# A decoder block on one Trainium2 core: its first projection taken by feature tiles instead of by output units

## The chip, the cores and the metric

The kernel runs on one core of one Trainium2 chip. The core has a matrix engine (TensorE, PE in the profile, with its weight loads as PEld), a vector engine (VectorE, DVE), an activation engine (ScalarE, ACT), a general engine (GpSimd, POOL) and a queue engine that issues the transfers (SyncE, SP), each with its own instruction stream, and sixteen DMA engines. The metric is the time of one execution in microseconds of the device, the median of several runs. Less is better.

## The reference, cut to what matters

Input is one sequence of 1024 positions with 1024 features and a conditioning vector `c`. Everything is float32.

```python
c_act = silu(c)
cond = c_act @ ada_w + ada_b                       # 1024 x 6144
shift1, scale1, gate1, shift2, scale2, gate2 = split(cond, 6)

h = rmsnorm(x, norm1_g) * (1 + scale1) + shift1
z = h @ w_in + b_in                                # 1024 x 2048
u, v, val, gate = split(z, [512, 1024, 1536])
y_a = spatial_gating_mixer(gelu(u), gelu(v), ...)  # layer norm of v, 128 x 128 mixing per head
y_b = conformer_conv_mixer(val, gate, ...)         # val*sigmoid(gate), 31-tap conv, group norm, silu
y = concat(rmsnorm(y_a), rmsnorm(y_b))
x = x + gate1 * (y @ w_out)

h2 = rmsnorm(x, norm2_g) * (1 + scale2) + shift2
g, up = split(h2 @ w_ffn_in, 2)                    # 1024 x 5632
x = x + gate2 * ((silu(g) * up) @ w_ffn_out)
return rmsnorm(x, norm_f_g) * (1 + scale_f) + shift_f
```

## The kernel before

Features lie on the 128 partitions, so `x` is eight tiles `x0` to `x7` of 128 features by 1024 positions. The positions are worked on in two halves of 512. A float32 product is made of three matmuls on values rounded to the fast matmul format: each operand is split into a rounded part (`hi`, a copy made by ACT) and the remainder (`lo`, a subtraction), and `mm3` (lines 588 to 592) adds `hi·hi`, `lo·hi` and `hi·lo` into one PSUM bank. `weights` (line 566) loads 128x1024 numbers of a weight, lets ACT make `wh` and an engine of the caller's choice make `wl` (line 574).

The first phase makes `val` and `gate` of the first half. It needs `h1_0_k`, the normed and modulated input of feature tile k, and for that the two condition columns of the tile: shift and scale. A column is a product of 128x1024 numbers of `ada_w` with `cact` summed along the row (`ada_cols`, line 546, a DVE instruction with an accumulator); the numbers are loaded into the four `ypad` tiles, which later hold the input of the convolution. `finish_shift` and `finish_scale` (lines 557, 561, 562) add the bias and the norm's gain, three DVE instructions of one column. `modulated` (lines 602, 612, 613) makes the tile: DVE multiplies `x` with scale and the inverse root `r1a`, ACT adds the shift and rounds, DVE makes the remainder.

Eight PSUM banks hold the eight results `p{j}_{vg}` (four column groups j of `val` and of `gate`) through the whole phase. The weights come in eight units of 128 columns over all 1024 input features (`wvg`), one for each bank, so a feature tile k can be used for the banks whose unit has arrived: tile 0 for j = 0, tile 1 for j = 0 and 1 and tile 0 for the new j = 1, and so on; from tile 3 on each tile goes into all eight banks. POOL makes the `wl` of these units. The loop over the last tile takes j in the order 3, 2, 0, 1, and `glu` (lines 660, 662) then empties the banks into `ypad` in that order.

After it follow, for the rest of the mixer: `u` of the first half (banks `pu`), the second norm (`rstd`, lines 628 to 647: ACT squares, a matmul with ones sums over the features, ACT and DVE make the inverse root `rt_n`, a matmul of line 641 spreads it over 128 rows), the second half's `h1`, `v`, the spatial mixing, the convolution (`cv`, lines 851 and 854, on DVE, six of its 31 taps by ACT and POOL in lines 845 and 846), its group norm (`gn`, line 871), the output projection. `v` has the positions on the partitions, so its bias cannot come with the activation; it is added by one more matmul to each of the eight groups (line 753), whose operands `vsel` and `vb` have 33 rows: row 0 carries the bias, row 32 its remainder. The feed-forward network (lines 904 to 1180) is a scheme of seven products `A`, `B`, `C` in place of eight; a part of its first matmuls (`ah`) is done ahead, in the middle of the mixer.

The order of the instructions on each engine is not the order of the code. `fix_order` (line 440) takes all instructions, simulates them with a table of costs (`duration`, line 122, and the class `Clock`, line 304) and keeps a list schedule: at each step the engine that is free first takes the ready instruction with the longest path behind it. Transfers take part as instructions of SP. `Slots` says which buffer a tile gets; memory that pools share in time is handed over by `hand_over`. The order so found is then fixed on each engine.

## Time and profile before

| | |
|---|---|
| median of 3 runs | 1009.9 us (1009.88 to 1010.12) |
| the profiled execution: its time | 1013.1 us |
| its span, first to last instruction | 1011.4 us |
| PE busy | 967.0 us, 96% |
| PEld busy | 776.3 us, 77% |
| DVE busy | 876.9 us, 87% |
| ACT busy | 466.0 us, 46% |
| POOL busy | 421.4 us, 42% |
| mean granted clock of PE | 0.990 |
| share of the chain that ended last: PE, DVE, DMA, ACT, issue | 82%, 7%, 5%, 3%, 2% |

The span is what the trace shows; the time of that execution is 1.7 us more, and 3.2 us above the median of the runs without a profile. An engine's busy share is a mean over the whole span, and the stages differ: the first phase lies between 24.44 us, where the first matmul of a bank `p` starts, and 80.96 us, where the first `pu` starts. The mean clock of 0.990 is made of long stretches at full speed and short ones near half of it, so it has to be read for a stretch and not for the run. In the rows below, the idle time in square brackets is that of the engine before the instruction, with what ended it.

### The profile page before, as it was taken

The page shows a single profiled execution, that of the slowest core. Times are in us where ns is not written, and L with a number is a line of the kernel's source. Part 1 is how long each engine was busy: PE and PEld are TensorE (multiplying, and loading weights), DVE is VectorE, ACT ScalarE, POOL GpSimd, SP SyncE. Part 2 cuts the span into 40 slices and gives each one's busy share as a digit, 9 for nine tenths or more (in the row PEclk, how much of TensorE's full clock was granted, in tenths as well). Part 3 has the DMA queues.
Part 4 walks back from the last instruction along what each step waited for, and adds up shares of the span by engine and source line. Part 5 has one row for each costly group of instructions (what it writes and reads, how often), then busy time and mean ns, then how long its engine had stood idle before and what let it go on. Part 6 is the DMA issues. An engine that isn't in the chain of part 4 may idle for free.

```text
span 1011.4 us, 13149 instructions
## 1 busy us (share of the span) xinstructions
PE 967.0 (96%) x4613; PEld 776.3 (77%) x4613; DVE 876.9 (87%) x1216; ACT 466.0 (46%) x727; POOL 421.4 (42%) x240
## 2 busy tenths in 40 slices
PE   3799899999999999999999999999999999999994
PEld 1587677778878877788887888888888788888873
DVE  5978999899999736499999999999978989969946
ACT  5237747653375364365432333333336437226426
POOL 2618698773727410385344555444543100000121
PEclk9899999999999999999999999999999999999997
DMA  9854063343556633583577767776748918415104
GB/s 340 324 191 146 21 212 101 106 132 106 158 195 199 198 115 108 185 309 107 177 229 250 248 223 247 243 249 216 253 173 289 357 49 268 142 32 176 33 0 167
DMA packets 73567, 183.89 MB, mean 182 GB/s; under 512 B 8188, under 2 KB 10492, under 8 KB 73502
## 3 DMA queue, kind: packets, MB, share of 16 engines
q1 hardware_dynamic: 73502, 183.06, 53.6%
q8 instruction: 36, 0.59, 0.2%
q14 instruction: 29, 0.24, 0.1%
HBM read 141.87 MB, written 41.16 MB: 181 GB/s over the span
## 4 chain that ended last, share of the span: by engine, by line
PE 82%; DVE 7%; DMA 5%; ACT 3%; issue 2%; POOL 1%; SPq 0%; ACTq 0%; DVEq 0%; POOLq 0%
PE B L913 28%; PE C L913 16%; PE ah L913 10%; PE A L913 3%; PE po L591 3%; PE po L590 3%; PE po L592 3%; PE p L590 2%; PE p L591 2%; PE p L592 2%; PE v L590 2%; PE v L591 1%; PE v L592 1%; DMA ypad<-ada 1%; DVE fa L906 1%
## 5 line engine op out<-in xcount | busy, mean ns | idle before, releaser
L913 PE MATMUL B<-h,w_f 128*128 128x512 f32 x816 | 189.5, 389 | 0.7 <-DVE x L1132 0.7
L913 PEld LDWEIGHTS B<-h,w_f 128*128 128x128 f32 x816 | 153.0, 188 | 32.9 <-DVE x L1132 1.1
L851 DVE SCALAR_TENSOR_TENSOR cv<-ypad,colt,cv 128x512 f32<-128x512 f32 x216 | 147.1, 746 | 0.1
L913 PE MATMUL B<-fa,w_d 128*128 128x512 f32 x528 | 126.5, 390 | 1.4 <-DVE fa L906 1.0
L913 PE MATMUL C<-h,w_f 128*128 128x512 f32 x528 | 123.7, 389 | 0.0
L913 PEld LDWEIGHTS B<-fa,w_d 128*128 128x128 f32 x528 | 98.7, 188 | 23.8 <-DVE fa L906 1.9
L913 PEld LDWEIGHTS C<-h,w_f 128*128 128x128 f32 x528 | 99.1, 188 | 20.6
L913 PE MATMUL ah<-h,wh_a 128*128 128x512 f32 x320 | 100.9, 393 | 0.2 <-ACT sg L660 0.2
L1194 POOL TENSOR_TENSOR sq_nf<-sq_nf,sq_nf 128x512 f32<-128x512 f32 x9 | 12.6, 1395 | 184.7 <-ACT sq_nf L1189 184.7
L905 ACT ACTIVATE w_f<-raw_f 128x512 fp32r<-128x512 f32 x68 | 42.4, 630 | 97.3 <-PE B L913 52.0
L905 ACT ACTIVATE w_d<-raw_d 128x512 fp32r<-128x512 f32 (+1 forms) x72 | 42.1, 593 | 86.5 <-PE B L913 37.3
L574 POOL TENSOR_TENSOR wl_a<-raw_a,wh_a 128x1024 fp32r<-128x1024 f32 x20 | 49.2, 2462 | 70.8 <-ACT wh_a L573 69.8
L1155 POOL TENSOR_TENSOR x<-x,up 128x512 f32<-128x512 f32 x20 | 34.9, 1744 | 96.0 <-ACT x L1154 96.0
L913 PEld LDWEIGHTS ah<-h,wh_a 128*128 128x128 f32 x320 | 59.9, 188 | 14.7 <-issue 1.5
L906 DVE TENSOR_TENSOR w_f<-raw_f,w_f 128x512 fp32r<-128x512 f32 x68 | 67.0, 990 | 1.4 <-ACT w_f L905 1.4
L913 PE MATMUL C<-fa,w_d 128*128 128x512 f32 (+1 forms) x273 | 64.6, 384 | 0.0
L913 PE MATMUL ah<-h,wl_a 128*128 128x512 f32 x160 | 62.7, 394 | 0.0
L590 PE MATMUL p<-h,wh_vg 128*128 128x512 f32 x128 | 53.4, 423 | 9.3 <-ACT h L612 8.6
L913 PEld LDWEIGHTS C<-fa,w_d 128*128 128x128 f32 x273 | 50.0, 188 | 10.8 <-issue 1.0
L574 POOL TENSOR_TENSOR wl_vg<-raw_vg,wh_vg 128x1024 fp32r<-128x1024 f32 x16 | 43.4, 2728 | 35.3 <-ACT wh_vg L573 35.3
L906 DVE TENSOR_TENSOR fa<-a,fa 128x512 fp32r<-128x512 f32 x77 | 54.0, 741 | 0.2 <-ACT fa L905 0.2
L1262 DVE SCALAR_TENSOR_TENSOR x<-B,cond,x 128x512 f32<-128x512 f32 x48 | 35.8, 747 | 20.2 <-PE B L913 20.0
(223 smaller groups left out, 2142.3 us busy)
## 6 DMA issues: line engine op xcount, KB each, us to landing
acts<-x SPq DMA_DIRECT2D x77, 256.0 KB, 3.0
a<-acts SPq DMA_DIRECT2D x77, 256.0 KB, 4.3
raw_f<-wf SPq DMA_DIRECT2D x32, 512.0 KB, 3.9
ada<-ada SPq DMA_DIRECT2D x24, 512.0 KB, 3.7
x<-ada SPq DMA_DIRECT2D x24, 512.0 KB, 3.5
...
```

Of the source, the lines that this page charges most:

```text
L574: lo_eng.tensor_tensor(lo, raw, hi.bitcast(F32), op=ALU.subtract)
L590: PE.matmul(acc, shi, mhi, start=start, stop=False)
L591: PE.matmul(acc, slo, mhi, start=False, stop=False)
L592: PE.matmul(acc, shi, mlo, start=False, stop=stop)
L851: V.scalar_tensor_tensor(accs[j], src, wc, accs[j], op0=ALU.mult, op1=ALU.add)
L905: A.activation(dst[:, 0, :], src, AF.Copy)
L906: lo_eng.tensor_tensor(dst[:, 1, :], src, dst[:, 0, :].bitcast(F32), op=ALU.subtract)
L913: last_mm = PE.matmul(bank[:, cols], s, m[:, cols], start=first and p == 0 and i == 0, stop=p == n - 1 and i == 2, skip_group_check=True)
L1155: G.tensor_tensor(g0, g0, up0, op=ALU.mult)
L1194: G.tensor_tensor(sums[half], sums[half], t, op=ALU.add)
L1262: V.scalar_tensor_tensor(xs[k][:, part], bank[:, cols], ccol(GATE2, k), xs[k][:, part], op0=ALU.mult, op1=ALU.add)
```

## The change

The first phase goes by feature tiles. A new input `wk` holds rows 128k to 128k+127 of `w_in[:, 1024:]`, so one load of 128x1024 numbers serves tile k for all eight banks. For each k the kernel makes the two condition columns, splits `wk[k]` (the remainder on DVE instead of POOL), makes the tile and takes its 24 matmuls, j = 0 to 3; `glu` empties the banks in that order. The three small DVE instructions of a tile become two ACT instructions of one column (`Identity` with scale and bias), with `gain` made once on DVE. The tile itself is made by DVE (x times r), ACT (times scale plus shift), ACT (rounding copy) and DVE (remainder). The first norm's squares are no longer added in pairs on DVE: each goes to a matmul of its own, and the warming square root stands behind the second Silu. The bias of `v` has 128 rows, of which rows 0 and 32 count as before.

In the scheduler, a transfer holds SP until its queue would run dry in `DMA_AHEAD` = 0.5 us, so that what is issued next is chosen later; a matmul that uses part of the array costs 0.09 or 0.12 us more where it follows one of the other kind; three PE durations differ; and memory that pools share is handed over at one moment, when all tiles of the earlier pools are free.

```diff
@@ Step, duration, Clock
+        self.partial = self.engine == "PE" and (self.reads[0].box[1] - self.reads[0].box[0] < P
+                                                or self.reads[1].width < P)
-            t = {128: 0.213, 32: 0.16}.get(m, 0.115)
+            t = {128: 0.219, 32: 0.068}.get(m, 0.109)
-            t = n / 600
+            t = 0.857
-            self.free["SP"] = t + DMA_ISSUE
+            self.free["SP"] = max(t + DMA_ISSUE, self.queue - LOAD_WAIT - DMA_AHEAD)
+        if s.engine == "PE" and s.partial != self.partial:
+            self.partial = s.partial
+            t += 0.09 if s.partial else 0.12
@@ Slots.hand_over
+        if self.in_use or not self.waits_for:
+            return []
@@ block_kernel
-        A.activation(cact[:, hs(h)], cb, AF.Silu)
+        silu = A.activation(cact[:, hs(h)], cb, AF.Silu).ins
     warm = const.tile([P, 1], F32, name="warm")
-    A.activation(warm, epst, AF.Sqrt)
+    with issue_after(silu):
+        A.activation(warm, epst, AF.Sqrt)
-    vb = front.tile([33, DA], F32R, name="vb")
-    vsel = front.tile([33, 1], F32R, name="vsel")
+    vb = front.tile([P, DA], F32R, name="vb")
+    vsel = front.tile([P, 1], F32R, name="vsel")
-        raw = tmp("vb_raw")[0:33]
-        nc.sync.dma_start(raw, vbias.partition_broadcast(33))
+        raw = tmp("vb_raw")
+        nc.sync.dma_start(raw, vbias.partition_broadcast(P))
-    r1a = rstd(x_half(0), D, "n1_0", (2, 2, 2, 2), V, True)
+    r1a = rstd(x_half(0), D, "n1_0", (1,) * 8, None, True)
+    gain = const.tile([P, KD], F32, name="gain")
+    V.scalar_tensor_tensor(gain, bcol(SCALE1, 0, KD), 1.0, colt[:, _OFF["norm1_g"]:_OFF["norm1_g"] + KD],
+                           op0=ALU.add, op1=ALU.mult)
     for k in range(KD):
-        ada_cols(SHIFT1 * 8 + k, dst=ypad[2 * k % 4][:, HALO:HALO + D])
-        ada_cols(SCALE1 * 8 + k, dst=ypad[(2 * k + 1) % 4][:, HALO:HALO + D])
-        if k < 4:
-            for vg in range(2):
-                w8[k, vg] = weights(wvg[2 * k + vg], f"vg{vg}_{k}", G, "act" if k >= 2 else "w")
-        finish_shift(SHIFT1, k, 1)
-        finish_scale(SCALE1, "norm1_g", k, 1)
-        h1[0][k] = modulated(0, k, r1a, SHIFT1, SCALE1, f"h1_0_{k}")
-        for j in range(min(k + 1, 4)) if k < KD - 1 else (3, 2, 0, 1):
-            for kk in range(k + 1) if (j == k) else (k,):
-                for vg in range(2):
-                    mm3(acc[j, vg], unit(w8[j, vg], kk), full(h1[0][kk]), kk == 0, kk == KD - 1)
-    for j in (3, 2, 0, 1):
+        for m, g in ((SCALE1, 0), (SHIFT1, 1)):
+            ada_cols(m * 8 + k, dst=ypad[(2 * k + g) % 4][:, HALO:HALO + D])
+        w_k = weights(wk[k], f"k{k}", V)
+        A.activation(ccol(SCALE1, k), ccol(SCALE1, k), AF.Identity, bias=gain[:, k:k + 1], scale=col("norm1_g", k))
+        A.activation(ccol(SHIFT1, k), ccol(SHIFT1, k), AF.Identity, bias=bcol(SHIFT1, k))
+        t = tmp(f"t_h1_0_{k}")
+        V.tensor_tensor(t, xs[k][:, hs(0)], r1a, op=ALU.mult)
+        A.activation(t, t, AF.Identity, bias=ccol(SHIFT1, k), scale=ccol(SCALE1, k))
+        h = h1[0][k] = act_tile(f"h1_0_{k}", 0)
+        A.activation(h[:, 0, :], t, AF.Copy)
+        V.tensor_tensor(h[:, 1, :], t, h[:, 0, :].bitcast(F32), op=ALU.subtract)
+        for j in range(4):
+            for vg in range(2):
+                mm3(acc[j, vg], unit(w_k, 4 * vg + j), full(h), k == 0, k == KD - 1)
+    for j in range(4):
         glu(j, 0, acc[j, 0], acc[j, 1])
-            PE.matmul(bank, vsel.broadcast_to([33, P]), vb, start=False, stop=True)
+            PE.matmul(bank, vsel.broadcast_to([P, P]), vb, start=False, stop=True)
```

On SP, the transfers that follow the first half of `x` stood in this order before (`ypad` gets columns of `ada_w`, `raw_vg` the units of the weight, `x0` to `x7` here are the second half of `x`, which only the second norm needs):

```order
L541 DMA ypad1_107<-ada 128x1024
L541 DMA ypad0_106<-ada 128x1024
L509 DMA colt_74<-cols 128x277
L541 DMA ypad3_109<-ada 128x1024
L541 DMA ypad2_108<-ada 128x1024
L568 DMA raw_vg0_0_177<-wvg 128x1024
L568 DMA raw_vg1_0_183<-wvg 128x1024
L568 DMA raw_vg0_1_207<-wvg 128x1024
L937 DMA x0_76<-xT 128x512
L937 DMA x1_77<-xT 128x512
L937 DMA x2_78<-xT 128x512
L937 DMA x3_79<-xT 128x512
```

and now (`raw_k` is the row block of tile k):

```order
L521 DMA colt_74<-cols 128x277
L554 DMA ypad0_106<-ada 128x1024
L554 DMA ypad1_107<-ada 128x1024
L581 DMA raw_k0_191<-wk 128x1024
L554 DMA ypad2_108<-ada 128x1024
L554 DMA ypad3_109<-ada 128x1024
L581 DMA raw_k1_233<-wk 128x1024
L554 DMA ypad0_106<-ada 128x1024
L554 DMA ypad1_107<-ada 128x1024
L581 DMA raw_k2_275<-wk 128x1024
L554 DMA ypad2_108<-ada 128x1024
L554 DMA ypad3_109<-ada 128x1024
```

The second half of `x` has moved behind the first phase's loads; each tile's two columns and its weight now stand side by side.

On DVE, in the middle of the first phase, the work for tiles 3 to 5 was this before (`ypad` rows are condition columns, `t_h1` and `h1` the tile and its remainder, the 128x1 rows bias and gain):

```order
L602 SCALAR_TENSOR_TENSOR t_h1_0_3_318<-x3_79,cond_105,r_n1_0_163 128x512
L613 SCALAR_TENSOR_TENSOR h1_0_3_320<-t_h1_0_3_318,cond_105,h1_0_3_320 128x512
L546 SCALAR_TENSOR_TENSOR ypad1_107,cond_105<-ypad1_107,cact_96 128x1024
L546 SCALAR_TENSOR_TENSOR ypad0_106,cond_105<-ypad0_106,cact_96 128x1024
L561 TENSOR_TENSOR cond_105<-cond_105,colt_74 128x1
L546 SCALAR_TENSOR_TENSOR ypad3_109,cond_105<-ypad3_109,cact_96 128x1024
L562 SCALAR_TENSOR_TENSOR cond_105<-cond_105,colt_74 128x1
L557 TENSOR_TENSOR cond_105<-cond_105,colt_74 128x1
L561 TENSOR_TENSOR cond_105<-cond_105,colt_74 128x1
L602 SCALAR_TENSOR_TENSOR t_h1_0_4_372<-x4_80,cond_105,r_n1_0_163 128x512
L546 SCALAR_TENSOR_TENSOR ypad2_108,cond_105<-ypad2_108,cact_96 128x1024
L613 SCALAR_TENSOR_TENSOR h1_0_4_374<-t_h1_0_4_372,cond_105,h1_0_4_374 128x512
```

and now:

```order
L725 TENSOR_TENSOR t_h1_0_3_325<-x3_79,r_n1_0_175 128x512
L587 TENSOR_TENSOR wl_k3_320<-raw_k3_317,wh_k3_319 128x1024
L559 SCALAR_TENSOR_TENSOR ypad0_106,cond_105<-ypad0_106,cact_96 128x1024
L729 TENSOR_TENSOR h1_0_3_328<-t_h1_0_3_325,h1_0_3_328 128x512
L559 SCALAR_TENSOR_TENSOR ypad1_107,cond_105<-ypad1_107,cact_96 128x1024
L725 TENSOR_TENSOR t_h1_0_4_367<-x4_80,r_n1_0_175 128x512
L587 TENSOR_TENSOR wl_k4_362<-raw_k4_359,wh_k4_361 128x1024
L559 SCALAR_TENSOR_TENSOR ypad2_108,cond_105<-ypad2_108,cact_96 128x1024
L729 TENSOR_TENSOR h1_0_4_370<-t_h1_0_4_367,h1_0_4_370 128x512
L559 SCALAR_TENSOR_TENSOR ypad3_109,cond_105<-ypad3_109,cact_96 128x1024
```

The small rows have gone to ACT, and each tile now has the weight's remainder `wl_k` on DVE: five rows for one tile.

On DVE around the second norm, whose inverse root is `rt_n1_1` and whose tiles are `t_h1_1`, the order before was (`cv` the convolution, `ada22` a later condition column):

```order
L851 SCALAR_TENSOR_TENSOR cv0_1_1130<-ypad1_107,colt_74,cv0_1_1130 128x512
L851 SCALAR_TENSOR_TENSOR cv0_0_1129<-ypad0_106,colt_74,cv0_0_1129 128x512
L546 SCALAR_TENSOR_TENSOR ada22_969,cond_105<-ada22_969,cact_96 128x1024
L851 SCALAR_TENSOR_TENSOR cv0_1_1130<-ypad1_107,colt_74,cv0_1_1130 128x512
L639 RECIPROCAL rt_n1_1_768<-rt_n1_1_768 128x128
L851 SCALAR_TENSOR_TENSOR cv0_0_1129<-ypad0_106,colt_74,cv0_0_1129 128x512
L851 SCALAR_TENSOR_TENSOR cv0_1_1130<-ypad1_107,colt_74,cv0_1_1130 128x512
L602 SCALAR_TENSOR_TENSOR t_h1_1_0_775<-x0_76,cond_105,ssq_n1_1_719 128x512
L851 SCALAR_TENSOR_TENSOR cv0_0_1129<-ypad0_106,colt_74,cv0_0_1129 128x512
L851 SCALAR_TENSOR_TENSOR cv0_1_1130<-ypad1_107,colt_74,cv0_1_1130 128x512
L851 SCALAR_TENSOR_TENSOR cv0_0_1129<-ypad0_106,colt_74,cv0_0_1129 128x512
L602 SCALAR_TENSOR_TENSOR t_h1_1_1_781<-x1_77,cond_105,ssq_n1_1_719 128x512
```

and now:

```order
L866 SCALAR_TENSOR_TENSOR cv0_1_1144<-ypad1_107,colt_74,cv0_1_1144 128x512
L559 SCALAR_TENSOR_TENSOR ada22_983,cond_105<-ada22_983,cact_96 128x1024
L866 SCALAR_TENSOR_TENSOR cv0_0_1143<-ypad0_106,colt_74,cv0_0_1143 128x512
L866 SCALAR_TENSOR_TENSOR cv0_1_1144<-ypad1_107,colt_74,cv0_1_1144 128x512
L866 SCALAR_TENSOR_TENSOR cv0_0_1143<-ypad0_106,colt_74,cv0_0_1143 128x512
L652 RECIPROCAL rt_n1_1_782<-rt_n1_1_782 128x128
L866 SCALAR_TENSOR_TENSOR cv0_1_1144<-ypad1_107,colt_74,cv0_1_1144 128x512
L866 SCALAR_TENSOR_TENSOR cv0_0_1143<-ypad0_106,colt_74,cv0_0_1143 128x512
L615 SCALAR_TENSOR_TENSOR t_h1_1_0_789<-x0_76,cond_105,ssq_n1_1_733 128x512
L615 SCALAR_TENSOR_TENSOR t_h1_1_1_795<-x1_77,cond_105,ssq_n1_1_733 128x512
L615 SCALAR_TENSOR_TENSOR t_h1_1_2_801<-x2_78,cond_105,ssq_n1_1_733 128x512
L615 SCALAR_TENSOR_TENSOR t_h1_1_3_807<-x3_79,cond_105,ssq_n1_1_733 128x512
```

The reciprocal stands after 21 convolution instructions instead of 22, and the tiles follow each other without convolution between them.

## Rows read from the trace of the kernel before

**Rows 1.** Windows by stage: window, length, busy time (count) per engine, PEclk, DMA share, GB/s

```profile
24.40:81.00 56.60, 50.48 (x193) 39.91 (x193) 46.35 (x67) 18.24 (x25) 22.10 (x9) 0.94 0.65 236
...
110.00:300.00 190.00, 189.12 (x1008) 145.70 (x1007) 181.14 (x265) 107.65 (x157) 128.84 (x66) 1.00 0.40 131
300.00:400.00 100.00, 97.56 (x512) 77.30 (x511) 69.52 (x99) 51.38 (x73) 34.26 (x19) 1.00 0.50 161
```

**Rows 2.** Timeline of PE, 24 to 106 us: start, duration, line, op, [idle before <-releaser]

```profile
24.44 0.79 PE L590 MATMUL p<-h,wh_vg 128*128 128x512 f32 x1 [3.19 <-ACT h L612]
...
27.66 0.80 PE L590 MATMUL p<-h,wh_vg 128*128 128x512 f32 x1 [0.71 <-ACT wh_vg L573]
...
36.81 0.50 PE L590 MATMUL p<-h,wh_vg 128*128 128x512 f32 x1 [2.49 <-ACT h L612]
...
42.93 0.80 PE L590 MATMUL p<-h,wh_vg 128*128 128x512 f32 x1 [2.88 <-ACT h L612]
...
80.96 0.39 PE L590 MATMUL pu<-h,wh_u 128*128 128x512 f32 x1
...
105.14 1.16 PE L641 MATMUL ssq_n<-rt_n,colt 128*128 128x128 f32 x8 [2.63 <-DVE rt_n L639]
```

**Rows 3.** Windows of tile p alone (first-phase matmuls), columns as in Rows 1 without POOL

```profile
24.44:31.86 7.42, 6.71 (x14) 4.57 (x15) 0.00 (x0) 0.00 (x0) 1.00 1.05 343
...
42.93:48.99 6.06, 6.06 (x15) 4.82 (x16) 0.00 (x0) 0.00 (x0) 0.51 0.55 190
48.99:80.96 31.97, 31.97 (x142) 26.27 (x140) 1.84 (x3) 2.59 (x4) 1.00 0.45 160
```

**Rows 4.** Timeline of DVE, columns as in Rows 2

```profile
53.89 0.75 DVE L602 SCALAR_TENSOR_TENSOR t_h<-x,cond,r_n 128x512 f32<-128x512 f32 x1
...
56.51 1.22 DVE L546 SCALAR_TENSOR_TENSOR ada<-ada,cact 128x1024 f32<-128x1024 f32 x1
...
81.89 1.40 DVE L854 TENSOR_SCALAR cv<-ypad,colt 128x512 f32<-128x512 f32 x2
...
104.15 0.94 DVE L639 RECIPROCAL rt_n<-rt_n 128x128 f32<-128x128 f32 x1
...
348.57 1.23 DVE L574 TENSOR_TENSOR wl_o<-raw_o,wh_o 128x1024 fp32r<-128x1024 f32 x1 [0.17 <-ACT wh_o L573]
```

**Rows 5.** Timeline of ACT, columns as in Rows 2

```profile
26.56 1.04 ACT L573 ACTIVATE wh_vg<-raw_vg 128x1024 fp32r<-128x1024 f32 x1
...
113.05 0.73 ACT L606 ACTIVATE t_h<-t_h,cond 128x512 f32<-128x512 f32 x1 [1.48 <-DVE t_h L602]
113.80 0.63 ACT L607 ACTIVATE h<-t_h 128x512 fp32r<-128x512 f32 x1
```

**Rows 6.** Windows within the first phase, columns as in Rows 1

```profile
24.40:42.90 18.50, 12.41 (x37) 8.63 (x37) 17.50 (x20) 4.20 (x6) 11.22 (x5) 0.98 1.03 383
42.90:54.00 11.10, 11.07 (x37) 8.96 (x38) 11.09 (x12) 2.82 (x3) 9.86 (x3) 0.73 0.61 216
54.00:70.00 16.00, 16.00 (x72) 13.27 (x71) 15.78 (x33) 5.83 (x9) 0.00 (x0) 1.00 0.67 234
```

**Rows 7.** DVE lines, 24.4 to 54 us: shapes, count, busy us, mean ns, idle before

```profile
L546 DVE SCALAR_TENSOR_TENSOR ypad<-ypad,cact 128x1024 f32<-128x1024 f32 x7 | 11.4, 1637 | 0.0
L613 DVE SCALAR_TENSOR_TENSOR h<-t_h,cond,h 128x512 fp32r<-128x512 f32 x4 | 7.1, 1801 | 0.8 <-ACT h L612 0.8
L602 DVE SCALAR_TENSOR_TENSOR t_h<-x,cond,r_n 128x512 f32<-128x512 f32 x4 | 5.1, 1276 | 0.1
```

**Rows 8.** Timeline of PE around one bias matmul of v

```profile
139.45 0.39 PE L592 MATMUL v<-wl_v,h 128*128 128x512 f32 x1
139.77 0.50 PE L753 MATMUL v<-vb,vsel 33*128 33x512 f32 x1
...
140.53 0.39 PE L591 MATMUL v<-wh_v,h 128*128 128x512 f32 x1
```

**Rows 9.** Lines of tile vb: count, ns min/median/max, first and last start

```profile
L753 PE MATMUL v<-vb,vsel x8: 491/498/498, 139.8 to 191.5; 33*128 33x512 f32 x8
```

More of the change, by code (lines that the diff above doesn't have):

```diff
@@ L68 @@
 DMA_ISSUE = 0.44
+DMA_AHEAD = 0.5
 class Step:
@@ L230, in __init__ @@
         below = layout(stacked)
+        self.stacked = {tag for tag, *_ in below}
         self.reuse = {(tag, k): [(t, j) for t, j, a, b in below if a < hi and lo < b]
@@ L239, in __init__ @@
         self.g = graph
-        self.free = {tag: [None if graph.reuse.get((tag, k)) else (0.0, []) for k in range(bufs)]
+        self.free = {tag: [None if (tag, k) in graph.reuse else (0.0, []) for k in range(bufs)]
                      for tag, bufs in graph.bufs.items()}
@@ L245, in __init__ @@
         self.waits_for = {new: list(old) for new, old in graph.reuse.items()}
+        self.in_use = sum(len(graph.order[tag]) for tag in graph.stacked)
         self.follows = []
@@ L287, in release @@
                 self.free[tag][self.taken[name][0]] = self.released[name], [name]
+                self.in_use -= tag in self.g.stacked
                 woken.append(tag)
@@ L291, in hand_over @@
     def hand_over(self):
+        if self.in_use or not self.waits_for:
+            return []
         woken = []
-        for (tag, k), old in list(self.waits_for.items()):
-            if all(self.next[t] == len(self.g.order[t]) and self.free[t][j] is not None for t, j in old):
-                del self.waits_for[tag, k]
-                if old:
-                    self.free[tag][k] = (max(self.free[t][j][0] for t, j in old),
-                                         [p for t, j in old for p in self.free[t][j][1]])
-                    woken.append(tag)
+        for (tag, k), old in self.waits_for.items():
+            if old:
+                self.free[tag][k] = (max(self.free[t][j][0] for t, j in old),
+                                     [p for t, j in old for p in self.free[t][j][1]])
+            else:
+                self.free[tag][k] = 0.0, []
+            woken.append(tag)
+        self.waits_for = {}
         return woken
@@ L309, in __init__ @@
         self.port = self.queue = 0.0
-        self.last = None
+        self.last, self.partial = None, False
     def run(self, s, t):
@@ L457, in block_kernel @@
 def block_kernel(ctx: ExitStack, tc: tile.TileContext, xT, c, ada, cols, vbias, bs, wsp,
-                 wv, wu, wvg, wo, wf, wfo, wfl, cst, out):
+                 wv, wu, wk, wvg, wo, wf, wfo, wfl, cst, out):
     nc = tc.nc
@@ L678, in load_mixer_operands @@
             nc.sync.dma_start(bst[e * 64:(e + 1) * 64], bs[e].partition_broadcast(64))
-        raw = tmp("vb_raw")[0:33]
-        nc.sync.dma_start(raw, vbias.partition_broadcast(33))
+        raw = tmp("vb_raw")
+        nc.sync.dma_start(raw, vbias.partition_broadcast(P))
         A.activation(vb, raw, AF.Copy)
         V.tensor_tensor(vb[32:33], raw[32:33], vb[32:33].bitcast(F32), op=ALU.subtract)
-        A.activation(vsel, col("sel_hl")[0:33], AF.Copy)
+        A.activation(vsel, col("sel_hl"), AF.Copy)
         nc.sync.dma_start(cstt, cst)
@@ L718, in block_kernel @@
-    first_phase_loaded = ada_dma[SCALE1 * 8 + KD - 1].ins
-    for j in (3, 2, 0, 1):
+    acc = {(j, vg): alloc[2 * j + vg](f"p{j}_{vg}") for j in range(4) for vg in range(2)}
+    gain = const.tile([P, KD], F32, name="gain")
+    V.scalar_tensor_tensor(gain, bcol(SCALE1, 0, KD), 1.0, colt[:, _OFF["norm1_g"]:_OFF["norm1_g"] + KD],
+                           op0=ALU.add, op1=ALU.mult)
+    for k in range(KD):
+        for m, g in ((SCALE1, 0), (SHIFT1, 1)):
[12 more added lines that the diff above has]
+                mm3(acc[j, vg], unit(w_k, 4 * vg + j), full(h), k == 0, k == KD - 1)
@@ L720, in block_kernel @@
+    first_phase_loaded = ada_dma[SHIFT1 * 8 + KD - 1].ins
+    for j in range(4):
         glu(j, 0, acc[j, 0], acc[j, 1])
@@ L1369 @@
     colv.update(sel_tok=part[:, None] == 32 * np.arange(4)[None, :], sel_grp=sel_grp.reshape(P, 16),
-                sel_hl=(part % 32 == 0)[:, None])
+                sel_hl=((part == 0) | (part == 32))[:, None])
     cst = np.concatenate([np.eye(P) - same, gind.reshape(P, 64)], axis=1).astype(np.float32)
@@ L1381 @@
         wu=units(w_in0[:, :512]),
+        wk=w_in0[:, 1024:].reshape(KD, P, D),
         wvg=vg,
```

4 lines of the change are left out of this document (removed).

## The prediction

> **What bounds the kernel now.** I read the windows by stage first [rows 1]. In the long middle PE leaves nothing: 189.12 of 190 us are busy from 110 to 300, and 97.56 of 100 from 300 to 400. So whatever this change gains must come from the stages where PE is idle or slow, or from PE instructions that become fewer or cheaper. The first phase is such a stage: from 24.4 to 81 PE is busy 50.48 of 56.6 us, at a mean clock of 0.94.
>
> Then I read PE's timeline there [rows 2]. The first matmul starts at 24.44, and three times PE then stands still for `h` or `wh_vg`: 0.71, 2.49 and 2.88 us. The windows of tile `p` show what lies between [rows 3]. After 48.99 PE runs 142 matmuls in 31.97 us, 0.225 each, the full rate. Two earlier stretches are slower: 14 in 6.71 busy us, 0.48 each, and 15 in 6.06 us, 0.40 each. For the second the row gives a granted clock of 0.51, near 1.2 of 2.4 GHz; it starts right after the idle 2.88 us. For the first the clock column reads 1.00 although its matmuls take twice the time, so there I trust the durations.
>
> Third, who made PE wait. DVE is busy 17.50 of 18.5 us from 24.4 to 42.9 and 11.09 of 11.1 up to 54, while POOL is busy 11.22 and 9.86 [rows 6]. In that stretch DVE's two-input instructions take 1637 ns (columns of `ada`), 1276 (`t_h`) and 1801 (`h`) on the mean [rows 7]; from 54 to 70, where POOL is busy 0.00 [rows 6], the columns take 1.22 us, and `t_h` at 53.89, as POOL ends, 0.75 [rows 4]. So the phase is held up early by DVE beside POOL's splits of the weights, and PE catches up on a backlog from 49 to 81. Both halves matter: tiles that come late first, and a backlog of matmuls that could not be done earlier.
>
> **First phase: its matmuls.** There are 8 tiles of 24, 192 as before. At 0.2275 a tile is 5.46 us of PE. DVE now has five instructions for a tile: two columns at 1.22, the weight's remainder at 1.23 (priced by `wl_o`, the same form), `t` and the remainder of `h` at 0.75 or less [rows 4]. The sum is 5.17, and somewhat less start to start, so DVE goes a little faster than PE needs. ACT has 1.04 + 0.73 + 0.63 [rows 5] and two single columns, under 3 us. A tile's three loads are 1.57 MB: 4.1 us at the 383 GB/s that the phase reaches while the transfers' share is 1.03; at 216 or 234 GB/s (shares 0.61 and 0.67, so not full) it would be 6.7 to 7.3 [rows 6]. I take the full rate, since SP now issues nothing but these loads. So PE should run through. The gaps of 0.71, 2.49 and 2.88 go: **6.1 us**. The second slow stretch comes after such a gap and goes with it: 6.06 − 15 × 0.225 = **2.7**. The first one follows the wait before 24.44 (3.19 us idle) and stays.
>
> **Its start.** Ahead of the first tile the norm's reciprocal stands behind two columns and not three, one 1.22 less [rows 4]; the pair sums are gone from DVE, but the square root for warming is now on the way; and the tile has a scaling and a copy on ACT where it had one pass, at most 0.73 + 0.63 more [rows 5]. I put the sum at 0, between −1.2 and +1.4. The first phase then ends about 72, against 80.96.
>
> **Hand-over to `u`.** `pu` needs a bank of the kind that `p2_0` has. Before, j = 2 was emptied second of four; now third, with its Sigmoid and `glu` nearer to the end. I charge **−0.4** (0 to −0.7).
>
> **The second norm.** PE waits 2.63 us at 105.14 for `rt_n` [rows 2], whose reciprocal starts at 104.15 [rows 4]. DVE starts the convolution at 81.89 and needs 22.3 us to that reciprocal. Now one convolution instruction and one column (`ada19`, which stands among the `glu`) fewer lie between, so some 20 us; with the start near 73.2 it comes at 93. PE has 21.5 us of work from its first `pu` to that point (80.96 to 102.5), so it arrives near 93.8 with a start at 72.4. Of the 2.63 little is left: **+2.3** (0, where ACT's square root or late loads of the second half of `x` hold it, to 2.6).
>
> **The bias of v.** Eight matmuls with 33 rows [rows 9]. Three steps from 139.45 to 140.53 take 1.08 us where three full ones take 0.68 [rows 8]: 0.40 extra each, **3.2 us** for eight, all in a stage where PE is the bound. With 128 rows the stationary tile has the shape of its neighbours. The bounds are 0, if the cost belongs to the change of operand or the bank's end, and 3.2.
>
> The Trainium skill has two rules that differ here. "TensorEngine Tiling (Array Packing)", Key Properties, says that a change of tiling mode drains TensorE; "TensorE: Matmul & The Clock Gate", Why this matters for your kernels, says that a single matmul with K = 32 takes the time of one with K = 128. By the second alone the edit would give nothing and the total would be 3.2 us higher; the 0.40 in the rows, on both sides of the short matmul, agrees with the first.
>
> **New waits later.** PE is early by 8.8 − 0.4 + 2.3 + 3.2 = 13.9 us by 200; DVE starts the convolution only 8.7 us earlier and has 1.7 less to do in it. From 110 to 300 it is busy 181.14 of 190 us [rows 1], so it has 8.9 us to catch up, and from 300 to 400 it is idle for 30. Some of PE's lead may wait for it in between: **−0.8** (0 to −4). The longer array switches and the other order of transfers move a few instructions in the feed-forward part, where PE waits for hardly anything: 0, plus or minus 1.5.
>
> **Sum.** 6.1 + 2.7 − 0.4 + 2.3 + 3.2 − 0.8 = **13.1 us**. The profiled span of 1011.4 would become 998.3. That execution's time is 3.2 above the median of the runs, and I take the difference from the median: 1009.9 − 13.1 = **996.8 us**.
>
> **Rivals.**
> *DVE keeps the lead it has.* If everything behind the convolution waits for DVE, the gain is only DVE's own, 8.7 + 1.7 = 10.4, and less if the remainder of `u`'s weights on POOL slows the last tiles. For it: 181.14 of 190 busy. Against: PE works ahead on `ah` in that stage, and idle DVE time follows. Time: about 1000. Chance 0.20.
>
> *Transfers bound the first phase.* At 216 to 234 GB/s a tile takes about 7 us instead of 5.46, and seven intervals add 10.8 us of gaps that eat up the 8.8 and the part of the second norm that hangs on them. What is left is the bias and a little of the rest. Time: about 1006. Against it stands 383 GB/s in the same phase [rows 6]. Chance 0.07.
>
> *DVE bounds the first phase, and the kernel is slower.* The split of the weights now stands in DVE's stream. If DVE's instructions kept the means they have beside POOL [rows 7], a tile would take 3 × 1.637 + 1.276 + 1.801 = 8.0 us; the last tile would start at 24.4 + 7 × 8.0 = 80.4 and the phase end at 85.8, 4.8 later. The convolution would start later by as much, and with DVE as the bound behind it the bias gives nothing: about 1014.7. It decides from 7.3 us for a tile, (80.96 − 24.44 − 5.46)/7. Against it: those durations come with POOL busy, and POOL's eight splits of this phase are what has been moved; at 0.00 POOL the rows show 1.22 and 0.75. Chance 0.06.
>
> The Trainium skill, "SBUF — State Buffer", Who interferes with whom, says that a DVE instruction with two SBUF inputs contends with a GpSimd instruction that reads SBUF, and that the loser blocks for the whole instruction. The trace agrees: 1637 against 1220 ns for one form. By that rule this rival needs work on GpSimd in the phase, and only the last tiles, beside the splits for `u`, would have it.
>
> **How the numbers follow.** The forecast has 0.62, with its own range 994 to 999.5 from the bounds of its terms. The three rivals have 0.20, 0.07 and 0.06; 0.05 is left for a larger gain, where the start is earlier and waits in the rest of the kernel go as well. The range 991.5 to 1003 holds the forecast and the first rival and leaves out the other two and the far end. About 0.2%, 2 us, is what a measurement of this kernel can tell from no change. Faster by more: 0.62 + 0.20 + 0.05 and nearly all of the second rival, 0.92; slower 0.06; the same 0.02.
>
> **What would show it.** In the profile after: `p` matmuls from about 24.4 to 72 with no idle over 0.5 us between them and one slow stretch only; DVE columns at 1.22 us in the whole phase; first `pu` near 72.4; under 0.5 us of idle before the spread of `rt_n`; the step of v's bias at 0.23 us. The forecast is wrong if tiles come more than 5.5 us apart, if the short clock comes back after a wait in the phase, or if PE in 90 to 300 has new waits for DVE of several us.

## The result and the profile after

The changed kernel takes 997.43 us (median of 4 runs, 996.41 to 999.47) against 1010.01 us of the kernel before in the same session (4 runs, 1009.88 to 1012.06). The ratio is 0.9873, with a 95% interval of 0.9851 to 0.9896: 12.6 us less, where 13.1 were forecast. Two later sessions gave ratios of 0.9855 and 0.9866 (below).

The profiled execution of the changed kernel has a span of 994.4 us, at a mean clock of 0.995. PE's timeline, to be read beside [rows 2] (start, duration, line, operation, idle time before and what ended it; the first and last matmul of the first phase, the first of `u`, the spread of the second norm):

```profile
24.22 0.80 PE L603 MATMUL p<-h,wh_k 128*128 128x512 f32 x1 [3.72 <-ACT h L728]
...
69.54 0.39 PE L603 MATMUL pu<-h,wh_u 128*128 128x512 f32 x1
...
91.51 1.16 PE L654 MATMUL ssq_n<-rt_n,colt 128*128 128x128 f32 x8
```

No row between 24.22 and 91.51 has an idle time of 0.2 us or more. The phase takes 45.3 us instead of 56.5, and the spread of the second norm, which had waited 2.63 us, waits no longer. The windows of tile `p` alone, to be read beside [rows 3] (window, length, busy time and count of PE, PEld, DVE and ACT, granted clock, DMA share, GB/s):

```profile
24.22:27.80 3.58, 3.58 (x8) 2.81 (x9) 0.00 (x0) 0.00 (x0) 1.00 0.87 302
27.80:69.54 41.74, 41.74 (x185) 34.36 (x183) 1.85 (x3) 1.95 (x3) 1.00 0.90 317
```

One slow stretch is left, of 8 matmuls where there had been 14 and 15; behind it stand 185 records in 41.74 us, 0.226 each. The clock column reads 1.00 for the slow row here too, so again it is the durations that tell. Transfers run at 317 GB/s and a share of 0.90: close to full, but not late.

DVE's lines in the first phase answer to [rows 7] (shapes, count, busy us, mean ns, idle before):

```profile
L559 DVE SCALAR_TENSOR_TENSOR ypad<-ypad,cact 128x1024 f32<-128x1024 f32 x12 | 14.5, 1217 | 0.0
L587 DVE TENSOR_TENSOR wl_k<-raw_k,wh_k 128x1024 fp32r<-128x1024 f32 x7 | 8.5, 1217 | 0.0
L729 DVE TENSOR_TENSOR h<-t_h,h 128x512 fp32r<-128x512 f32 x8 | 7.3, 909 | 0.4 <-ACT h L728 0.4
L725 DVE TENSOR_TENSOR t_h<-x,r_n 128x512 f32<-128x512 f32 x6 | 4.1, 684 | 0.0
```

A column costs 1217 ns instead of 1637, `t` 684 instead of 1276. The 909 of `h` holds one instruction of 2.48 us, that of the last tile, beside POOL's first split for `u`.

Last, two of the stages of [rows 1], moved to where the same work now lies:

```profile
100.00:287.00 187.00, 186.51 (x1006) 146.10 (x1005) 183.51 (x272) 106.23 (x156) 126.00 (x65) 1.00 0.42 137
287.00:387.00 100.00, 97.92 (x515) 78.00 (x514) 65.79 (x92) 49.73 (x69) 32.77 (x20) 1.00 0.48 156
```

PE is as full as before in the stage behind the phase, and DVE, busy 183.51 of 187 us, is fuller; it had to follow, and did.

The two profiled executions differ by 17.0 us in span, the medians by 12.6. To read such a ledger rightly both kernels were profiled again (e9 and e12 below). The times at which the same work starts, in us (`rs` is a small tile ahead of `v`):

| start of | before | before again | after | after again (e12) | lead of e12 over before again |
|---|---|---|---|---|---|
| first `p` | 24.44 | 24.62 | 24.22 | 24.23 | 0.4 |
| first `pu` | 80.96 | 78.81 | 69.54 | 69.20 | 9.6 |
| `rs` | 132.43 | 128.98 | 117.36 | 117.29 | 11.7 |
| last bias of `v` | 191.55 | 188.10 | 173.30 | 173.23 | 14.9 |
| first `ah` | 294.70 | 291.24 | 277.25 | 277.18 | 14.1 |
| first `B` | 466.61 | 463.18 | 448.22 | 448.11 | 15.1 |
| first `B` of the second product | 772.20 | 768.76 | 755.45 | 756.82 | 11.9 |
| span | 1011.4 | 1007.6 | 994.4 | 994.0 | 13.6 |

So by the second pair 9.6 of the gain come in the first phase, 2.1 up to `v`, 3.2 in `v`; 0.8 are lost up to `ah`, 1.0 comes back up to `B`, 3.1 are lost in the first product of the feed-forward network, and 1.7 come back behind it. By the first pair, which has the profile that the forecast was read from, the first phase gives 11.4.

The 0.8 that are lost between the last bias and `ah` are no wait. Here is that stretch, first before, then after, with the columns of [rows 1]:

```profile
191.55:294.70 103.15, 102.86 (x575) 81.59 (x574) 96.61 (x133) 50.59 (x69) 61.53 (x30) 1.00 0.44 145
173.30:277.25 103.95, 103.95 (x575) 81.04 (x574) 101.07 (x148) 50.30 (x69) 59.66 (x30) 1.00 0.45 143
```

PE has no idle time left there, and the same 575 records take 1.1 us more. In the timelines PE changes 19 times between matmuls on a part of the array (rows with `128*64` or `128*32`) and full ones before, and 28 times after; a full 128x512 matmul behind such a group mostly takes a step of 0.34 us instead of 0.23. Nine more changes at some 0.1 us each are an estimate of about 1 us. No run changes this alone.

### The profile page after: what moved, and what is told of

Same layout as the page of the kernel before. It is cut to its first block, busy times and chain, and to the rows that moved or that the text cites. A ratio compares the mean times of both kernels' runs of the same rounds, so it can differ in the third digit from the quotient of the medians.

```text
span 994.4 us, 13218 instructions
## 1 busy us (share of the span) xinstructions
PE 961.9 (97%) x4645; PEld 773.6 (78%) x4645; DVE 855.2 (86%) x1197; ACT 474.0 (48%) x751; POOL 391.4 (39%) x232
## 4 chain that ended last, share of the span: by engine, by line
PE 83%; DVE 10%; issue 2%; ACT 2%; DMA 1%; POOL 0%; SPq 0%; ACTq 0%; DVEq 0%; POOLq 0%
PE B L928 24%; PE C L928 14%; PE ah L928 11%; PE p L603 3%; PE po L603 3%; PE po L604 3%; PE po L605 3%; PE p L604 3%; PE p L605 3%; PE A L928 3%; DVE w_f L921 2%; PE v L604 2%; PE v L603 1%; PE pu L605 1%; PE v L605 1%
## 5 line engine op out<-in xcount | busy, mean ns | idle before, releaser
L928 PEld LDWEIGHTS ah<-h,wh_a 128*128 128x128 f32 x320 | 59.9, 188 | 15.1 <-issue 1.4
L921 DVE TENSOR_TENSOR fa<-a,fa 128x512 fp32r<-128x512 f32 x77 | 54.2, 743 | 1.7 <-ACT fa L920 1.7
L920 ACT ACTIVATE fa<-a 128x512 fp32r<-128x512 f32 x77 | 46.0, 626 | 8.8 <-DMA a<-acts 5.7
L921 DVE TENSOR_TENSOR w_d<-raw_d,w_d 128x512 fp32r<-128x512 f32 (+1 forms) x72 | 47.8, 673 | 1.4 <-ACT w_d L920 1.4
```

Of the source, the lines that this page charges most:

```text
L920: A.activation(dst[:, 0, :], src, AF.Copy)
L921: lo_eng.tensor_tensor(dst[:, 1, :], src, dst[:, 0, :].bitcast(F32), op=ALU.subtract)
L928: last_mm = PE.matmul(bank[:, cols], s, m[:, cols], start=first and p == 0 and i == 0, stop=p == n - 1 and i == 2, skip_group_check=True)
```

## The experiments

The times of one kernel spread by 2 to 6 us in a session (the kernel before: 1007.0 to 1013.3 over 18 runs of one session), so ratios to the kernel before are given with their intervals, and where two kernels ran in one session their ratios are compared.

**e1, e2 and e5: the bias of v.** In e1 the changed kernel gets its 33 rows back:

```diff
-    vb = front.tile([P, DA], F32R, name="vb")
-    vsel = front.tile([P, 1], F32R, name="vsel")
+    vb = front.tile([33, DA], F32R, name="vb")
+    vsel = front.tile([33, 1], F32R, name="vsel")
-            PE.matmul(bank, vsel.broadcast_to([P, P]), vb, start=False, stop=True)
+            PE.matmul(bank, vsel.broadcast_to([33, P]), vb, start=False, stop=True)
```

> The changed kernel with v's bias over 33 rows again; all else as in the change. Theory (the short matmul costs 0.40 us extra each, on PE's critical path): 8 x 0.40 = 3.2 us more, about 1000.6 against 997.4, the step of the bias about 0.5 us longer in the trace. Rival A (the cost belongs to the change of operand and not to the rows): the same time as the changed kernel. Rival B (the lead is lost to DVE behind it): the step is longer but the end moves less than 1 us.

It took 1002.59 us, ratio 0.9922 (0.9904 to 0.9940): some 5 us more than the changed kernel, more than any theory had. The scheduler had seen another shape and a smaller load and had moved instructions on all engines. The trace has waits that the changed kernel does not have, two of them here (PE's timeline):

```profile
92.15 1.16 PE L654 MATMUL ssq_n<-rt_n,colt 128*128 128x128 f32 x8 [0.72 <-DVE rt_n L652]
...
206.39 0.79 PE L603 MATMUL p<-h,wh_vg 128*128 128x512 f32 x1 [1.58 <-ACT sg L673]
```

So e1 mixes the bias with a new order and does not decide. e2 is the kernel before with the reverse edit, whose order does not change:

> The kernel before with v's bias over 128 rows and nothing else; the order on every engine is that of the kernel before. Theory: 3.2 us less, 1006.8 against 1010.0. Rival A: no change. Rival B (lost to DVE, which is busy 181 of 190 us there): under 1 us less.

1007.06 us, ratio 0.9973 (0.9959 to 0.9987): 2.7 us less, 1.3 to 4.1. Theory's 3.2 lies inside, rival A's zero does not, and rival B's end below 1 us does not either. Its profile, beside the second profile of before, shows where the time is won: `rs` starts at 128.91 and 128.98, the last bias of `v` 2.9 us earlier (185.22 against 188.10), `ah` 3.2 earlier (288.01 against 291.24), and the span is 3.7 shorter (1003.9). So the gain arises in `v` and reaches the end. e5 is e1 made clean: loads and tiles stay at 128 rows, the scheduler is told to take the short matmul for a full one, and only the matmul's operands are cut.

```diff
-        self.partial = self.engine == "PE" and (self.reads[0].box[1] - self.reads[0].box[0] < P
+        self.partial = self.engine == "PE" and (self.reads[0].box[1] - self.reads[0].box[0] not in (33, P)
-            PE.matmul(bank, vsel.broadcast_to([P, P]), vb, start=False, stop=True)
+            PE.matmul(bank, vsel[0:33].broadcast_to([33, P]), vb[0:33], start=False, stop=True)
```

> The changed kernel, in which v's bias matmul uses rows 0 to 32 of its operands and nothing else changes; loads and the order on every engine are those of the changed kernel. Theory: 8 x 0.40 = 3.2 us more than the changed kernel, about 1000.6, with the step of the bias 0.40 longer. Rival A (the cost belongs to the change of operand): the same. Rival B (PE's lead is lost to DVE anyway): the step is longer and the end moves by less than 1 us.

1000.11 us, ratio 0.9890 (0.9870 to 0.9910), against 0.9855 (0.9835 to 0.9875) of the changed kernel in that session: 3.5 us, whose interval is some 3 us to either side. Here the trace says more than the time. PE around the second bias, in e5:

```profile
132.30 0.39 PE L605 MATMUL v<-wl_v,h 128*128 128x512 f32 x1
132.62 0.50 PE L768 MATMUL v<-vb,vsel 33*128 33x512 f32 x1
133.05 0.50 PE L603 MATMUL v<-wh_v,h 128*128 128x512 f32 x1
133.38 0.39 PE L604 MATMUL v<-wh_v,h 128*128 128x512 f32 x1
```

and in the changed kernel:

```profile
130.07 0.39 PE L605 MATMUL v<-wl_v,h 128*128 128x512 f32 x1
130.29 0.40 PE L768 MATMUL v<-vb,vsel 128*128 128x512 f32 x1
130.53 0.39 PE L603 MATMUL v<-wh_v,h 128*128 128x512 f32 x1
130.76 0.40 PE L604 MATMUL v<-wh_v,h 128*128 128x512 f32 x1
```

The three steps, the short matmul's and those to either side, take 1.08 us with 33 rows and 0.69 with 128. Same operands, same bank, same order: the cost belongs to the rows. Of the profile's later end not all is the bias: from `rs` to the last bias e5 takes 2.7 us more than the changed kernel of that session (e8), but it comes to `rs` 1.3 later already, mostly through a wait of 1.63 us for `rt_n` at the second norm.

**e3: the scheduler alone.** The kernel before with the whole scheduler of the changed one:

```diff
+DMA_AHEAD = 0.5
-            self.free["SP"] = t + DMA_ISSUE
+            self.free["SP"] = max(t + DMA_ISSUE, self.queue - LOAD_WAIT - DMA_AHEAD)
...
```

> The kernel before with the scheduler of the changed one (transfers put in order when their queue runs dry, costs of the matmuls, hand-over of memory) and the old first phase by units and the old bias. Theory (the gain is the first phase by tiles with POOL's splits gone, 8.8 us, and the bias): at most 3 us less than 1010, since DVE still works beside POOL; PE still stands still for 2 us or more after the first tiles. Rival (the order of the transfers is what made the tiles late): 8 us less or more, about 1002, with the gaps in the first phase gone.

1014.38 us, ratio 1.0045 (1.0028 to 1.0062): slower, which neither theory nor rival had. PE in its first phase:

```profile
34.54 0.78 PE L603 MATMUL p<-h,wl_vg 128*128 128x512 f32 x1 [1.34 <-POOL wl_vg L586]
...
37.82 0.80 PE L603 MATMUL p<-h,wl_vg 128*128 128x512 f32 x1 [2.07 <-POOL wl_vg L586]
...
40.47 0.80 PE L602 MATMUL p<-h,wh_vg 128*128 128x512 f32 x1 [1.43 <-ACT h L624]
```

and DVE there:

```profile
21.01 2.83 DVE L614 SCALAR_TENSOR_TENSOR t_h<-x,cond,r_n 128x512 f32<-128x512 f32 x1
23.76 3.38 DVE L558 SCALAR_TENSOR_TENSOR ypad<-ypad,cact 128x1024 f32<-128x1024 f32 x1
27.07 2.85 DVE L625 SCALAR_TENSOR_TENSOR h<-t_h,cond,h 128x512 fp32r<-128x512 f32 x1
```

The weight's units stand earlier in the queue, POOL is busy with seven of their splits without a break from 17.65 to 37.77, and DVE's two-input instructions stretch to about 3 us beside them; the first column behind that stretch, at 37.77, takes 1.21. PE now waits for POOL itself as well (6.4 us of idle in the phase, first `pu` at 80.72). The rival that the transfers' order alone had made the tiles late falls. Of the loss, 1.6 us lie in the first product of the feed-forward network, which takes 307.2 us from first `B` to first `B` of the second product where before again takes 305.6.

**e4: one line of the scheduler undone.**

```diff
-            self.free["SP"] = max(t + DMA_ISSUE, self.queue - LOAD_WAIT - DMA_AHEAD)
+            self.free["SP"] = t + DMA_ISSUE
```

> The changed kernel with one line of the scheduler undone: a transfer holds SP only for its issue, so that transfers are put in order as early as buffers are free. The second half of x, the mixing weights and some weights of later tiles (over 3 MB) then stand ahead of the columns of tile 2. Theory (the transfers' order carries the first phase, as 3 MB at 383 GB/s take 8 us): PE waits some 5 to 8 us before tile 2 and has a second slow stretch of 2.7; about 1005. Rival (the loads are far enough ahead, DVE and PE set the phase): the same time within 1 us.

999.11 us, ratio 0.9899 (0.9880 to 0.9917). PE's timeline:

```profile
37.01 0.50 PE L603 MATMUL p<-h,wh_k 128*128 128x512 f32 x1 [1.72 <-ACT h L728]
...
49.92 0.50 PE L603 MATMUL p<-h,wh_k 128*128 128x512 f32 x1 [1.56 <-ACT h L728]
...
62.84 0.50 PE L603 MATMUL p<-h,wh_k 128*128 128x512 f32 x1 [1.71 <-ACT h L728]
...
69.99 0.50 PE L603 MATMUL p<-h,wh_k 128*128 128x512 f32 x1 [1.06 <-ACT h L728]
```

The gaps are there, 6.0 us in all, spread over the tiles and not at tile 2 alone; the phase starts 2.4 earlier (21.84) and the first `pu` comes at 76.09, 6.6 later. Here DVE waits for the loads of `ypad` (2.22 us before 31.05, 0.79 before 33.08). The second slow stretch of the theory does not come: behind each of these four waits PE goes on at 0.23 from its second matmul. In the profile the lag lasts: 6.9 us at the first `B`, 5.5 in the span of 999.9. But this execution was 2.5 us above the median of its kernel, and the ratios differ by only 0.0026 (the changed kernel's 0.9873 is of another session), with intervals that overlap. So the transfers' order matters to the phase, as the theory has it; the time of 1005 did not come, the rival's 1 us is not clearly kept either, and how much reaches the end is not settled. By tiles and with the late order, the kernel still gains 10 us, though its phase takes 54.3 us, as long as in the second profile of before (54.2); the lead of 2.7 us over that profile at the first `pu` grows to 8.1 at the first `B`. So the shorter phase is not all of the gain.

**e6: the weights' remainders on POOL again.**

```diff
-        w_k = weights(wk[k], f"k{k}", V)
+        w_k = weights(wk[k], f"k{k}", G)
```

> The changed kernel with the weights' remainders of the first phase on POOL again (eight of 128x1024), everything else by tiles as in the change. Theory (DVE's two-input instructions block beside POOL's): DVE's columns take 1.6 to 3.4 us again, a tile 6.5 to 8 us, PE stands still in the phase, first pu at 78 to 84 instead of 69.5; 1004 to 1010. Rival (the order by tiles alone carries the gain; DVE is freed of 1.23 us a tile): first pu at 69.5 or earlier, the same time within 1.5 us.

1000.02 us, ratio 0.9886 (0.9868 to 0.9904), against 0.9855 of the changed kernel in the session. DVE's lines from 24 to 70 us, and one row of POOL's timeline:

```profile
L559 DVE SCALAR_TENSOR_TENSOR ypad<-ypad,cact 128x1024 f32<-128x1024 f32 x12 | 27.3, 2309 | 0.0
L729 DVE TENSOR_TENSOR h<-t_h,h 128x512 fp32r<-128x512 f32 x7 | 11.4, 1622 | 0.0
...
L725 DVE TENSOR_TENSOR t_h<-x,r_n 128x512 f32<-128x512 f32 x5 | 5.6, 1117 | 0.0
```

```profile
40.35 12.15 POOL L587 TENSOR_TENSOR wl_k<-raw_k,wh_k 128x1024 fp32r<-128x1024 f32 x4 [3.59 <-ACT wh_k L586]
```

The same column costs 2309 ns instead of 1217, and PE stands still for 5.1 us up to the first `pu`, which ends a phase of 52.0 us (21.28 to 73.29) instead of 45.1:

```profile
53.07 0.50 PE L603 MATMUL p<-h,wh_k 128*128 128x512 f32 x1 [2.45 <-ACT h L728]
...
73.29 0.50 PE L603 MATMUL pu<-h,wh_u 128*128 128x512 f32 x1 [2.08 <-ACT sg L673]
```

That is the theory's mechanism, but smaller: 6.5 us for a tile is the lower end of what it gave, the first `pu` comes before its 78 to 84 and the time below its 1004 to 1010. The start came 3 us earlier, as `c` is loaded first in this order, and POOL's eight splits are spread out from 21 to 52 us, so that not every DVE instruction meets one. And 2.1 of the 5.1 are not a late tile: there `u` waits for a bank until ACT's sigmoid has read it.

**e7 and e11: PE kept busy ahead of the phase.**

```diff
+        if k == 0:
+            with issue_after(last["rstd"]):
+                for _ in range(8):
+                    PE.matmul(acc[0, 0], w_k[0][:, 0:P], w_k[0][:, 0:H], start=True, stop=True)
```

> The changed kernel with eight matmuls of 128x512 whose result is overwritten, put on PE right behind the spread of the first norm (20.5 us), where PE stands still for 3.7 us before the first matmul of the phase. Theory (the slow first stretch of 8 matmuls at 0.40 is the clock after that idle time): the phase's first matmuls go at 0.23 or change over sooner, 8 x 0.17 = 1.4 us less, about 996. Rival (the start is slow for another reason, operands or the transfers): the first 8 matmuls of the phase at 0.40 as before, no gain.

> The kernel of e7_warm once more, for more runs beside the changed kernel on one chip. Theory: 1.8 us less than the changed kernel, as the first pu came at 67.82 instead of 69.60. Rival: the time won at the start is lost again where PE waits for DVE (second norm, feed-forward), under 0.5 us less.

PE's timeline in e7:

```profile
20.07 3.00 PE L733 MATMUL p<-wh_k 128*128 128x512 f32 x8
24.14 0.50 PE L603 MATMUL p<-h,wh_k 128*128 128x512 f32 x1 [1.08 <-ACT h L728]
24.48 0.40 PE L604 MATMUL p<-h,wl_k 128*128 128x512 f32 x1
24.71 0.40 PE L603 MATMUL p<-h,wh_k 128*128 128x512 f32 x1
...
67.82 0.39 PE L603 MATMUL pu<-h,wh_u 128*128 128x512 f32 x1
```

The added matmuls take the slow steps, eight in 3.00 us, and the phase runs at 0.23 from its second matmul on. From its first matmul to the first `pu` it takes 43.7 us instead of 45.1, the 1.4 of the theory; the first `pu` comes 1.8 earlier than in the changed kernel of that session (69.60). So the slow start hangs on PE's idle time ahead of it, and the rival falls. That it is the clock is read from the durations, near twice the full rate's as in the stretch of [rows 3] with a granted clock of 0.51; the clock column itself stays at 1.00. In time the two sessions give 0.9851 (0.9828 to 0.9874) and 0.9850 (0.9833 to 0.9867) against 0.9855 and 0.9866: over 8 runs a median of 996.7 us, over 12 of the changed kernel 997.2. The sign fits, but it is not clear of the spread. In the traces the lead is not lost at the second norm, as the rival has it: at the first `B` both are some 2.4 us ahead of the changed kernel of their session. e7's span is 2.6 shorter; e11 loses the lead in the feed-forward part, whose first product takes 310.8 us there, with waits for DVE (1.77 us in one), and its span is 1.1 longer.

**e8, e9 and e12: both kernels again.**

> The changed kernel itself, for more runs and a second profile. Expected: 997.4 within 1 us; first pu at 69.5 within 0.5 us; a span between 994.4 and 997.5, by which the spread of a single profile is read.

> The kernel before itself, for a second profile. The two profiles that are compared differ in span by 17.0 us, the medians by 12.6. If the first profile of before was a long execution, this one has a span near 1008 to 1009, with the missing 2 to 3 us in the first phase (first pu before 80.96) and in the waits of PE and not in the count of matmuls. If the difference of the profiles is real, the span is 1011 again.

> The changed kernel once more, beside the warm kernel and e10_costs_back on one chip: 996.5 to 997.5.

The changed kernel: 996.61 us, ratio 0.9855 (0.9835 to 0.9875), and 997.55 us, ratio 0.9866 (0.9849 to 0.9883), with spans of 994.3 and 994.0 in the profiles, just under the 994.4 to 997.5 that was expected, and the first `pu` at 69.60 and 69.20. The kernel before, profiled again, has a span of 1007.6. PE's timeline there:

```profile
27.77 0.80 PE L590 MATMUL p<-h,wh_vg 128*128 128x512 f32 x1 [0.65 <-ACT wh_vg L573]
...
36.93 0.50 PE L590 MATMUL p<-h,wh_vg 128*128 128x512 f32 x1 [2.65 <-ACT h L612]
...
43.05 0.50 PE L590 MATMUL p<-h,wh_vg 128*128 128x512 f32 x1 [1.43 <-ACT h L612]
...
101.71 1.16 PE L641 MATMUL ssq_n<-rt_n,colt 128*128 128x128 f32 x8 [1.35 <-DVE rt_n L639]
```

The third gap is 1.43 us where [rows 2] have 2.88, and the second norm waits 1.35 instead of 2.63. The windows of tile `p` around the second and third gap:

```profile
36.90:43.05 6.15, 4.70 (x13) 3.21 (x14) 0.00 (x0) 0.00 (x0) 0.72 1.02 409
43.05:50.00 6.95, 6.95 (x31) 5.77 (x32) 0.00 (x0) 0.00 (x0) 1.00 0.53 200
```

Here the slow clock comes behind the second gap and ahead of the third, where PE would have waited for the next tile anyway, and behind the third all matmuls are at full speed; in [rows 3] it came behind the third and held up matmuls that were ready. The phase of this execution takes 54.2 us and not 56.5. The profile that the forecast was read from was the longer of the two, by 3.8 us in span, of which 2.2 are there by the first `pu` and 3.5 by `rs`.

**e10: the scheduler's costs of matmuls undone.**

```diff
-            t = {128: 0.219, 32: 0.068}.get(m, 0.109)
+            t = {128: 0.213, 32: 0.16}.get(m, 0.115)
-            t += 0.09 if s.partial else 0.12
+            t += 0.0
```

> The changed kernel with the scheduler's costs of matmuls as before (no cost of changing between full and part of the array, the old three durations); transfers, first phase and bias as in the change. My expectation, as the forecast gave the reorder 0 plus or minus 1.5: 997 within 1.5 us. Rival (the costs keep part-array matmuls together, 74 changes instead of 86, at 0.1 to 0.2 us each, and put waits elsewhere): 1.5 to 3 us more.

998.28 us, ratio 0.9876 (0.9859 to 0.9893), against 0.9866 in the session: 1 us more, no difference that can be told. But the trace shows how a lead is lost. With these costs `c` is loaded first, the phase starts at 19.21 and ends at 64.20, 5 us before the changed kernel's; then PE runs ahead of the squares of the second norm:

```profile
82.29 0.42 PE L648 MATMUL ssq_n<-sq_n,ones 128*32 128x128 f32 x8 [2.20 <-ACT sq_n L641]
83.52 1.18 PE L648 MATMUL ssq_n<-sq_n,ones 128*32 128x128 f32 x16 [0.80 <-ACT sq_n L641]
```

In the stretch from 64 to 90 us the clock of 0.93 shows a slow stretch behind these waits:

```profile
64.00:90.00 26.00, 23.00 (x153) 18.09 (x152) 22.37 (x31) 19.69 (x28) 19.86 (x12) 0.93 0.51 182
```

At `rs` 1.5 us are left of the 5, at the first `ah` none (277.26 against 277.18). On the other side PE has no wait in its first product of the feed-forward network: 305.05 us from first `B` to first `B` of the second product, where the changed kernel takes 307.2 and 308.7 with waits such as (one row of each profile)

```profile
616.78 3.06 PE L928 MATMUL B<-h,w_f 128*128 128x512 f32 x12 [0.88 <-DVE x L1147]
...
618.20 3.02 PE L928 MATMUL B<-h,w_f 128*128 128x512 f32 x12 [1.50 <-DVE x L1147]
```

## Why the prediction was right

The time came out as forecast, 997.43 for 996.8, and so did the mechanism in the main: the waits of the first phase are gone with POOL's work beside DVE, and the bias of `v` costs what the rows said. That the two times lie within 0.7 us is in part luck, as the sizes show step by step:

- *The gaps in the phase*, 6.1: gone, in every profile of the changed kernel. In the second profile of before they are 4.7, so the term was right for the execution it was read from and 1.4 high for the other.
- *The second slow stretch*, 2.7: gone. In the second profile of before it costs 13 matmuls 4.70 − 13 × 0.226 = 1.8.
- *The first slow stretch*, forecast to stay: it shrank from 14 matmuls to 8. 14 in 6.71 became 8 in 3.58 and 6 at 0.226, 1.8 us that the forecast did not have. This is the term it sized wrongly. The gap of 0.71 us that had interrupted PE soon after its start is gone as well; that the stretch is shorter for it fits the profiles (before, before again and e2 have the gap and the long stretch, the changed kernel neither), but no run removes that gap alone. e7 shows that the 8 that are left come of the idle time ahead of them.
- *DVE's and the transfers' rate*: DVE's columns take 1217 ns in the whole phase. The rival that DVE bounds the phase had its condition right, POOL beside DVE: e6 brings that back by one letter, and it costs 6.9 us of the phase, 2.1 of them at the hand-over to `u`. Even then the kernel stays 11 us faster than before. That is not the rival's whole case, which has the splits on DVE and its slow instructions as well; no run has both, so its 1014.7 is not tested. The rival that transfers bound the phase does not hold at 317 GB/s; e4 shows that it would begin to if the second half of `x` went first.
- *The hand-over to `u`*, −0.4: nothing; the first `pu` follows the last `p` at 0.23. Where the last tile comes late the term is there: 0.35 in e4, 2.08 in e6.
- *The second norm*, +2.3: the wait is 0.46 and less in the three profiles of the changed kernel, against 2.63 and 1.35. It is not gone for good: e5, whose order is the same up to there, waits 1.63.
- *The bias of v*, 3.2: 2.7 (1.3 to 4.1) by e2, 3.5 by e5, and 3.2 in the ledger between `rs` and the last bias. Between the two rules that the prediction takes from the Trainium skill, the row of the trace decided rightly. The cost on both sides of the short matmul agrees with "TensorEngine Tiling (Array Packing)", Key Properties. The statement on a single matmul in "TensorE: Matmul & The Clock Gate", Why this matters for your kernels, does not describe one of 33 rows that stands between full ones. That it is a drain of TensorE no run shows; the runs show the cost.
- *New waits for DVE from 110 to 300*, −0.8: the ledger loses 0.8 between the last bias and `ah`, but not to DVE and to no wait at all: PE is busy 103.95 of 103.95 us, and the same matmuls take longer, with more changes between part and full array. The number came out for another reason than the one given: this is luck. From 110 to 300 the one wait of 0.2 us or more is of 0.49, for ACT, where 0.21 had been. So the rival that DVE keeps the lead falls too; DVE's 183.51 of 187 us shows that it was near, and its own lead was larger than that rival had it, as the convolution starts 10.3 us earlier (71.57 against 81.89) and not 8.7.
- *The feed-forward part*, 0 plus or minus 1.5: the sum from `ah` to the end is −0.4 in the ledger, but it is made of larger parts. The first product takes 1.6 to 3.1 us longer, with more and longer waits for DVE. That it goes with the order, and not with the change of the first phase, fits e3, which has the old phase and 1.6 of it, and e10, which has the new phase and none (one profile each).

So the sum came out right, but not each term. In the first phase idle time and slow matmuls were forecast to give 6.1 + 2.7 = 8.8. In the first pair of profiles they give 6.1 of idle and 5.1 of PE's busy time (50.4 to 45.3), and the first `pu` comes 11.4 earlier: 2.6 more than forecast. In the second pair they give 4.7 and 4.5 (49.5 to 45.0), 9.6 with the earlier start. Of the busy time 1.8 is the first slow stretch and up to 1 us single longer steps (0.32 to 0.45 us) that came with the waits; the forecast had neither. Against the second pair, then, two errors nearly cancel: gaps counted 1.4 too high, slow matmuls 1.8 too low. Behind the phase 2.1, 3.2, −0.8 and −0.4 stand there against 2.3, 3.2, −0.8 and 0.

The way from the sum to the time is the other piece of luck. The terms were read from an execution 3.2 us above the median, and were taken off the median. From profile to profile the forecast was 998.3, and the span measured 994.4: 17.0 us less and not 13.1. That the terms were too small against that execution is what lets their sum fit an ordinary one.
